# Two first products interleaved per tile of x, squares on ACT, and a third pair of output tiles ahead of the last head's transposes

## The chip, the cores and the metric

One core of a Trainium2 chip runs one launch of the kernel. The metric is the device time of a launch in microseconds, as a median of several runs. A profile is one more execution, recorded by the hardware profiler; its "span" goes from its first to its last instruction. The engines are PE (matmul and transpose), PEld (weight loads, beside PE), DVE, ACT, POOL and SP (which here only issues DMAs).

## What is computed

Two layers on 512 tokens of 1024 features, float32 (shapes fixed, one batch). Cut to what matters here:

```python
for l in range(2):
    n = rmsnorm(h, attn_norm[l])
    u, v_sgu, q, k, v_att = split(n @ w_in[l])           # 512 columns each
    y_sgu = gelu(u) * (tril(w_s) @ groupnorm(gelu(v_sgu)) + b_s)   # per chunk of 128 tokens
    y_att = diff_attention(rope(q), rope(k), v_att)      # 4 heads, two softmaxes each, then rmsnorm
    h = h + concat(y_sgu, y_att) @ w_out[l]
    h = h + (silu(conv(g)) * conv(v)) @ w_down[l]        # g, v = rmsnorm(h) @ w_up[l]; 2816 wide
return rmsnorm(h, final_norm)
```

## The kernel before

The residual lies on chip as eight tiles `hT` of [128 features, 512 tokens]. Each float32 operand of a matmul is split into a high and a low part, and each product takes three matmuls (high x high, high x low, low x high). The 1/rms of a token is applied after the product, so products can start on `g * x` before the sum of squares is known.

**Weights.** `block(i)` streams the weights in blocks of [128, 1024], two ahead (`AHEAD = 2`), through three buffers each of `raw`, `wh`, `wl`: SP's DMA into `raw`, a cast on ACT into `wh`, a subtraction on POOL (in the mixer) into `wl`. A `wh` buffer comes free when PE has finished the block before in it. Of layer 0, blocks 0 to 19 belong to `w_in`, 20 to 27 to `w_out`.

**Products.** `feat_step` multiplies one tile of x with two 128-column tiles of weights (6 matmuls of 512 columns); `tok_gemm` makes tokens the rows (12 matmuls of 256 columns per tile). `products()` is a generator, one yield per tile: gate values `vs` of groups 0 and 1 (blocks 0, 1), queries `q` (2, 3), gate values of groups 2 and 3 (4, 5), keys `k` (6, 7), attention values `va` (8, 9), and on. `run(steps, n)` takes n steps and after each the next piece of element-wise work from the queue `due`: for gate values gelu and squares on ACT, sums, a reciprocal root (`gr`, `rsqrt`) and scaling on DVE, split into `vg` parts; for q and k `rope`: shuffle and product on DVE, two POOL operations (`q_0sh`, `q_0t`), a split on ACT and DVE. All four PSUM banks of `ps_mm` turn around in these products.

**Order.** Where `pinned[0]` is true, each engine's instructions run as written; engines are coupled by semaphores alone. An engine that waits holds everything behind it.

**Opening.** `block(0)` brings x and the blocks 0 and 1 in 16 DMAs; each tile of x is scaled and split (`gh_a` on ACT, `gl_a` on DVE), its square is made and added on POOL (tiles 0 to 3) or made on ACT (4 to 7); the rotary tables are small DVE operations. Then come the sums (`norm.sums`: four transposes `ss_a`, `rcol_a` on DVE), and a row of 1/rms (`norm.rows`: `sr_a`).

**End of the mixer.** `project()` sums the first four tiles of the output projection (`pairs`, 16 steps; inputs in the order ya0, ya1, ya2, ys0 to ys3, ya3, blocks 20 to 23) between the attention units. After its 14th step the last head's output is normed on DVE (`out_norm`, tile `o`), transposed on PE (`ot`), split (`yah`, `yal`), and the rest of the steps follow. `residual` adds each finished tile to `hT` and feeds the next norm (`gh_f`, `gl_f`, square, sum), one tile after the other. Tiles 4 and 5, then 6 and 7, are two further `feat_gemm` (blocks 24, 25 and 26, 27).

Of the kernel before, what the change touches and what calls it, by code (L numbers as in the profile page):

```python
# [21 lines left out]
P = 128  # L22
# [20 lines left out]
# columns of the packed per-partition parameters  # L43
# [9 lines left out]
# 2 pi in pieces of 12 bits, so that their products with integers below 2**12 are exact  # L53
# [16 lines left out]
def trunk(ctx: ExitStack, tc, a, out):  # L70
# [24 lines left out]

    def tr_bank(name):
# [21 lines left out]
    pe, act, dve, gps = Ordered(nc.tensor), Ordered(nc.scalar), Ordered(nc.vector), Ordered(nc.gpsimd)  # L118
    mm, transpose = pe.matmul, pe.transpose

    # ---- residual stream, features on partitions
# [3 lines left out]
    # an early activation, so that the table's load is not in the way  # L125
# [4 lines left out]
    # TensorE works on zeros until the inputs come, so that its clock is up by then  # L130
# [6 lines left out]
    # ---- the weights' stream: each chunk comes once and is split into two exact parts  # L137
# [12 lines left out]
    AHEAD = 2  # L150

    def block(i):
        while len(loaded) <= min(i + AHEAD, len(specs) - 1):
# [8 lines left out]
            if j < KD // 4:  # L162
                # the first blocks come in pieces, between the tiles of x
                for k in range(4):
                    m = 4 * j + k
                    c = slice(k * 256, (k + 1) * 256)
                    nc.sync.dma_start(out=hT[m], in_=a["xT"][m])
                    nc.sync.dma_start(out=raw[:, c], in_=specs[j][:, c])
                    if m < 2:
                        dve.tensor_copy(h[:, c], raw[:, c])  # L170
                    norm.scaled(m)
                    if m >= 2:
                        act.copy(h[:, c], raw[:, c])
                    dve.tensor_sub(lo[:, c], raw[:, c], h.bitcast(F32)[:, c])
                    if m < 4:
                        norm.squared(m, True)
            else:
                nc.sync.dma_start(out=raw, in_=specs[j])
                act.copy(h, raw)
                mixer = j % (len(specs) // DEPTH) < 28  # L180
                eng = gps if mixer and j > 1 or j % 3 == 1 else dve
                eng.tensor_sub(lo, raw, h.bitcast(F32))
            loaded.append((h, lo))
        return loaded[i]

    def kept(j, n):
        """a block of the last products, which are done for one half of the tokens after the other"""
# [25 lines left out]
    def feat_gemm(banks, xs):  # L213
        """banks[j] = W[:, j]^T x; features out. Yields after each tile of x."""
# [5 lines left out]

    def tok_gemm(banks, xs):
        """x^T W for 256 columns; tokens out, two tiles of them in a bank"""
        for k, (xh, xl) in enumerate(xs):
# [3 lines left out]
            last = k == len(xs) - 1  # L227
            for t in range(NT):
                ts = slice(t * P, (t + 1) * P)
                o = banks[t // 2][:, t % 2 * 256 : t % 2 * 256 + 256]  # L230
                mm(o, xh[:, ts], h[:, c], start=k == 0 and t % 2 == 0, stop=False)
                mm(o, xh[:, ts], lo[:, c], start=False, stop=False)
                mm(o, xl[:, ts], h[:, c], start=False, stop=last and t % 2 == 1)
# [10 lines left out]
    # work on finished products, spread over the steps that follow them  # L244
# [9 lines left out]
    # ---- constants  # L254
# [9 lines left out]
    # ---- rotary tables, [feature, token]  # L264
# [5 lines left out]
    def rotary_tables():  # L270
        W = NT * HALF
        posf = sm.tile([P, NT], F32, tag="posf", name="posf", bufs=1)
        v = nc.vector
        v.tensor_copy(posf, posi)
        T = lambda n: sm.tile([P, W], F32, tag=n, name=n, bufs=1)
# [6 lines left out]
        )  # L282

        def turns(name, unit):
            k = T(name)
            v.tensor_scalar(k, r, 1.0 / (2.0 * math.pi) / unit, MAGIC, op0=ALU.mult, op1=ALU.add)
            v.tensor_scalar(k, k, MAGIC, unit, op0=ALU.subtract, op1=ALU.mult)
            return k

        def less(k, c):  # L290
            v.scalar_tensor_tensor(r, k, -TWO_PI[c], r, op0=ALU.mult, op1=ALU.add)

        k1 = turns("k1", 2.0**24)
# [25 lines left out]
        nc.scalar.activation(sn, r, AF.Sin)  # L319
        nc.scalar.activation(cs, cs, AF.Sin)  # L320
        for nm, src, dst, fill in (("c", cs, CT, 1.0), ("s", sn, ST, 0.0)):
            wide = tp.tile([P, 514], F32, tag="t", name=f"wide{nm}")[:, :S]
            nc.gpsimd.memset(wide, fill)
# [19 lines left out]
    def rsqrt(x, n, name):  # L343
        """x**-0.5 of a few columns: a guess from the exponent, then Newton's steps; x is lost"""
# [11 lines left out]
    # ---- RMS norm over features: g * h in two parts now, 1/rms of each token later  # L356
    class Norm:
# [17 lines left out]
        def squared(self, m, on_pool=False):  # L375
            sq = self.acc if m == 0 else tmp(f"sq{m}_{self.tag}")
            if on_pool:
                gps.tensor_mul(sq, hT[m], hT[m])
            else:
                act.activation(sq, hT[m], AF.Square)  # L380
            if m > 0:
                (dve if m == KD - 1 or m > 4 and self.tag == "a0" else gps).tensor_add(self.acc, self.acc, sq)

        def sums(self):
            """1/rms, a column for each tile of tokens"""
# [8 lines left out]
        def rows(self):  # L394
            """1/rms, a row on every partition"""
# [20 lines left out]
    block(0)  # L416
    for m in range(4, KD):
        norm.squared(m)
    rotary_tables()
    nc.sync.dma_start(out=par[:, C_CW:], in_=a["par"][:, C_CW:])  # L420
    for l in range(DEPTH):
        lam_init = 0.8 - 0.6 * float(np.exp(-0.3 * l))
        xs = norm.parts
        # ---- per-layer small parameters
        lamv = tmp(f"lamv{l}", 4 * HD).rearrange("p (v d) -> p v d", d=HD)
        nc.sync.dma_start(out=lamv, in_=a["lam"][l].rearrange("(v d) -> v d", d=HD).partition_broadcast(P))
        bsb = lp.tile([P, NG, P], F32, tag="bsb", name=f"bsb{l}")
        nc.sync.dma_start(out=bsb, in_=a["b_s"][l].partition_broadcast(P))
        wsp = tmp(f"wsp{l}").rearrange("p (g q) -> p g q", g=NG)
        nc.sync.dma_start(out=wsp, in_=a["w_sT"][l])  # L430

        def small():
            # lambda, on every partition
# [12 lines left out]
        # spatial weights: [q, g, p], zero where p < q  # L446
# [632 lines left out]
```

## Time and profile before

| | |
|---|---|
| median of 3 runs | 1157.69 us (1156.96 to 1157.77) |
| span of the profiled execution | 1155.4 us |
| PE busy | 1123.3 us, 97% |
| DVE, ACT, POOL busy | 685.9, 475.3, 416.3 us |

The profiled execution has no time of its own beside its span; the median of the runs is 2.3 us above it, which is what lies around a span. The rows further on start with the time in us from the span's start and the duration; a bracket at a row's end is the idle time of that engine ahead of it and what ended that. Matmuls overlap, so the distance between starts is what one costs, not its printed duration.

### The profile page before, as it was taken

What the parts mean: (1) busy time and instruction counts of PE and PEld (TensorE: products, weight loads), DVE (VectorE), ACT (ScalarE), POOL (GpSimd) and SP (SyncE); (2) the same over time, 40 slices, a digit from 0 to 9 for tenths busy, and PEclk for the clock granted to TensorE, in tenths of its full rate; (3) what the DMA queues carried; (4) which work ended last, traced back from release to release, by engine and by line L of the source; (5) the groups of instructions that cost most, each with busy time, mean ns of one, the idle gap of its engine ahead of it and who ended that gap; (6) DMA issues with size and microseconds to landing.
All of it is one profiled execution on the core that took longest, in us unless ns stands there. A gap on an engine that the chain in (4) does not pass through costs nothing.

```text
span 1155.4 us, 14800 instructions
## 1 busy us (share of the span) xinstructions
PE 1123.3 (97%) x5637; PEld 941.8 (82%) x5637; DVE 685.9 (59%) x1253; ACT 475.3 (41%) x797; POOL 416.3 (36%) x318
## 2 busy tenths in 40 slices
PE   7899998999999999999999999999999999999996
PEld 6787887888888888888889788778888888888886
DVE  8768786475665226764338688745666622565634
ACT  4345554443443223444344545544344321344351
POOL 5475423522232113143456752352323311232351
PEclk8999999999999999999999999999999999999999
DMA  6222212223323322323232211123322332233222
GB/s 206 80 73 92 73 47 72 93 92 93 108 91 99 102 91 92 109 82 91 101 106 91 92 55 56 55 73 110 106 95 91 91 110 92 91 100 101 75 90 73
DMA packets 33351, 105.24 MB, mean 91 GB/s; under 512 B 3968, under 2 KB 7424, under 8 KB 33280
## 3 DMA queue, kind: packets, MB, share of 16 engines
q1 hardware_dynamic: 32848, 104.27, 28.1%
q8 instruction: 44, 0.72, 0.3%
q14 instruction: 27, 0.22, 0.1%
q10 hardware_dynamic: 432, 0.03, 0.0%
HBM read 102.19 MB, written 2.10 MB: 90 GB/s over the span
## 4 chain that ended last, share of the span: by engine, by line
PE 80%; DVE 9%; POOL 3%; issue 3%; ACT 3%; DMA 0%; SPq 0%; DVEq 0%; POOLq 0%; ACTq 0%
PE g L116 21%; PE v L116 21%; PE dn L116 18%; PE wo L116 6%; PE u L116 4%; PE q L116 3%; PE dl L116 2%; PE sc L116 1%; PE vs L116 1%; PE mx L116 1%; PE av L116 1%; ACT wh L116 1%; DVE y L116 1%; POOL wl L116 1%; DVE s L116 1%
## 5 line engine op out<-in xcount | busy, mean ns | idle before, releaser
L116 POOL TENSOR_TENSOR wl<-raw,wh 128x1024 fp32r<-128x1024 f32 (+1 forms) x103 | 245.8, 2389 | 567.3 <-ACT wh L116 557.4
L116 ACT CAST wh<-raw 128x1024 fp32r<-128x1024 f32 (+2 forms) x200 | 198.5, 996 | 366.4 <-issue 195.1
L116 DVE TENSOR_TENSOR wl<-raw,wh 128x1024 fp32r<-128x1024 f32 (+2 forms) x99 | 123.8, 1250 | 129.0 <-ACT wh L116 129.0
L116 PE MATMUL g<-gh_f,wh 128*128 128x512 f32 x352 | 137.2, 390 | 0.0
L116 PE MATMUL v<-gh_f,wh 128*128 128x512 f32 x352 | 137.2, 390 | 0.0
L116 PE MATMUL v<-gh_f,wl 128*128 128x512 f32 x352 | 137.1, 389 | 0.0
L116 PE MATMUL g<-gh_f,wl 128*128 128x512 f32 x352 | 137.1, 389 | 0.0
L116 PE MATMUL v<-gl_f,wh 128*128 128x512 f32 x352 | 137.0, 389 | 0.0
L116 PE MATMUL g<-gl_f,wh 128*128 128x512 f32 x352 | 137.0, 389 | 0.0
L116 DVE SCALAR_TENSOR_TENSOR cv<-up_cv,par,cv 128x512 f32<-128x512 f32 x88 | 74.3, 891 | 8.0 <-ACT cv L116 7.7
L116 PEld LDWEIGHTS v<-gh_f,wl 128*128 128x128 f32 x352 | 66.1, 188 | 13.7
L116 PEld LDWEIGHTS g<-gh_f,wl 128*128 128x128 f32 x352 | 66.1, 188 | 13.7
L116 PEld LDWEIGHTS v<-gl_f,wh 128*128 128x128 f32 x352 | 66.1, 188 | 13.7
L116 PEld LDWEIGHTS g<-gl_f,wh 128*128 128x128 f32 x352 | 66.1, 188 | 13.6
L116 PEld LDWEIGHTS v<-gh_f,wh 128*128 128x128 f32 x352 | 66.1, 188 | 13.6
L116 PEld LDWEIGHTS g<-gh_f,wh 128*128 128x128 f32 x352 | 66.1, 188 | 13.6
L116 DVE SCALAR_TENSOR_TENSOR cg<-up_cg,par,cg 128x512 f32<-128x512 f32 x88 | 71.1, 855 | 6.8 <-ACT cg L116 6.3
L116 DVE TENSOR_TENSOR up_cv<-v,rstd_f 128x512 f32<-128x512 f32 x44 | 30.2, 692 | 67.5 <-PE v L116 67.5
L116 DVE TENSOR_TENSOR up_cg<-g,rstd_f 128x512 f32<-128x512 f32 x44 | 30.0, 692 | 53.7 <-PE g L116 53.1
L116 ACT ACTIVATE s<-s,mn 128x128 f32<-128x128 f32 (+3 forms) x64 | 35.5, 556 | 58.9 <-DVE mn L116 58.9
L116 DVE TENSOR_TENSOR hT<-dn,hT 128x512 f32<-128x512 f32 x28 | 19.1, 691 | 47.5 <-PE dn L116 47.5
L116 ACT ACTIVATE cg<-cg 128x512 f32<-128x512 f32 x44 | 27.7, 630 | 46.7 <-DVE cg L116 46.6
(575 smaller groups left out, 2624.2 us busy)
## 6 DMA issues: line engine op xcount, KB each, us to landing
raw<-in_w_up SPq DMA_DIRECT2D x88, 512.0 KB, 3.4
raw<-in_w_dn SPq DMA_DIRECT2D x40, 512.0 KB, 3.5
raw<-in_w_in SPq DMA_DIRECT2D x38, 512.0 KB, 3.5
raw<-in_w_out SPq DMA_DIRECT2D x16, 512.0 KB, 3.4
hT<-in_xT SPq DMA_DIRECT2D x8, 256.0 KB, 4.2
raw<-in_w_dn SPq DMA_DIRECT2D x8, 256.0 KB, 3.3
out<-y SPq DMA_DIRECT2D x8, 256.0 KB, 2.3
raw<-in_w_in SPq DMA_DIRECT2D x8, 128.0 KB, 4.1
```

The lines of the kernel that those rows point to most:

```text
L116: return lambda *args, **kw: pin(getattr(self.engine, op)(*args, **kw))
```

## The change

Four parts, the last two in both layers.

1. `opening()` replaces the split inside `block`: per tile of x three DMAs instead of two (x, a piece of block 0 or 1, a piece of block 2 or 3; 24 in all), and `both_first()` does per tile the 12 matmuls of `vs` and the 6 of `q`. Blocks 4 and 5 come after tiles 5 and 7. The second gate values use the two banks of the scores.
2. All squares of x are made on ACT and added on DVE; blocks 4 to 6 get their low part on DVE. POOL has no work on x left. The rotary table's steps are spread, two after each tile, the rest after `norm.sums`.
3. `project()` stops after 12 of 16 steps. Tiles 4 and 5 (`late`, in the scores' banks) take their first six inputs ahead of the last head's transposes; then come the last two inputs of all six tiles.
4. Only after that come the residuals: six in a row, then tiles 6 and 7.

```diff
+    def opening():
+        first = [[], []]
+        for m in range(KD):
+            sync.dma_start(out=hT[m], in_=a["xT"][m])
+            c = slice(m % 2 * 256, m % 2 * 256 + 256)
...
+            for b, (r, h, lo) in enumerate(tiles):
+                spec = specs[2 * b + m // 4]
+                sync.dma_start(out=r[:, c], in_=spec[:, m % 4 * 256 : (m % 4 + 1) * 256])
...
+            norm.squared(m)
+            if m > 0:
+                for _ in range(2):
+                    next(rotary)
+            if m == 5:
+                loaded.extend([None] * 4)
+                AHEAD[0] = 0
+                block(4)
+        block(5)
+        AHEAD[0] = 2
...
-                eng = gps if mixer and j > 1 or j % 3 == 1 else dve
+            eng = gps if (j > 6 if mixer else j % 3 == 1) else dve
...
+            def steps():
+                for k, x in enumerate(xs):
+                    tok_step(vb, x, first[0][k], k == 0, k == KD - 1)
+                    yield
+                    feat_step(qb, x, first[1][k], 0, k == 0, k == KD - 1)
+                    yield
...
+        def project_last(k):
+            for c in range(2):
+                feat_step(pairs[c], mixed[k], final[0], (2 * c + k - KD + 2) * 256, False, k == KD - 1)
...
-        run(steps, 1)
+        run(steps)
+
+        mixed = [ya[0], ya[1], ya[2], ys[0], ys[1], ys[2], ys[3], None]
+        late = [sc_bank(f"wo{4 + j}_{l}") for j in range(2)]
+        more = feat_gemm(late, mixed)
+        AHEAD[0] = 1
+        run(more, 6)
+        AHEAD[0] = 2
         end.out_turn()
         end.out_high()
         end.out_low()
-        run(steps)
+        mixed[-1] = ya[3]
+        project_last(KD - 2)
+        run(more, 1)
+        project_last(KD - 1)
         flush()
...
         for c in range(2):
             residual(c, pairs[c])
-        for c in range(2, 4):
-            banks = [mm_bank(f"wo{2 * c + j}_{l}") for j in range(2)]
-            run(feat_gemm(banks, mixed))
-            residual(c, banks)
+        run(more)
+        residual(2, late)
+        banks = [mm_bank(f"wo{6 + j}_{l}") for j in range(2)]
+        run(feat_gemm(banks, mixed))
+        residual(3, banks)
```

PE, start of layer 0, before: tile 1 of x (`gh1`) follows tile 0 (`gh0`), both for `vs` alone (`wh0`, `wl0` are the parts of block 0).

```order
L116 MATMUL vs1_0_0_289<-wh0_128,gh0_a0_133 128x256
L116 MATMUL vs1_0_0_289<-wl0_129,gh0_a0_133 128x256
L116 MATMUL vs1_0_0_289<-wh0_128,gl0_a0_134 128x256
L116 MATMUL vs0_0_0_288<-wh0_128,gh1_a0_142 128x256
L116 MATMUL vs0_0_0_288<-wl0_129,gh1_a0_142 128x256
```

The same place now (`oh1`, `ol1` are the parts of block 2):

```order
L119 MATMUL vs1_0_0_306<-oh0_0_129,gl0_a0_139 128x256
L119 MATMUL q0_0_307<-gh0_a0_138,oh1_0_132 128x512
L119 MATMUL q0_0_307<-gl0_a0_139,oh1_0_132 128x512
L119 MATMUL q0_0_307<-gh0_a0_138,ol1_0_133 128x512
L119 MATMUL q1_0_308<-gh0_a0_138,oh1_0_132 128x512
L119 MATMUL q1_0_308<-gl0_a0_139,oh1_0_132 128x512
L119 MATMUL q1_0_308<-gh0_a0_138,ol1_0_133 128x512
L119 MATMUL vs0_0_0_305<-oh0_0_129,gh1_a0_148 128x256
```

Six matmuls of the queries moved between two tiles of the gate values.

POOL, layer 0, from the turned queries to the turned keys, before (`wl9`, `wl10` are low parts of weight blocks, `wsl0` of the spatial weights):

```order
L116 TENSOR_TENSOR q0_1t1_599<-q0_1t1_599,q0_1sh_597 128x512
L116 TENSOR_TENSOR wl7_605<-raw7_603,wh7_604 128x1024
L116 TENSOR_TENSOR wl8_670<-raw8_668,wh8_669 128x1024
L116 AFFINE_SELECT wsp0_280<-wsp0_280 128x512
L116 TENSOR_TENSOR wsl0_283<-wsp0_280,wsh0_282 128x512
L116 TENSOR_TENSOR wl9_729<-raw9_727,wh9_728 128x1024
L116 TENSOR_TENSOR wl10_771<-raw10_769,wh10_770 128x1024
L116 TENSOR_TENSOR k0_0sh_787<-k0_0sh_787,Sr0_516 128x512
```

The same place now:

```order
L119 TENSOR_TENSOR wl8_670<-raw8_668,wh8_669 128x1024
L119 AFFINE_SELECT wsp0_297<-wsp0_297 128x512
L119 TENSOR_TENSOR wsl0_300<-wsp0_297,wsh0_299 128x512
L119 TENSOR_TENSOR wl9_713<-raw9_711,wh9_712 128x1024
L119 TENSOR_TENSOR q0_0sh_723<-q0_0sh_723,Sr0_618 128x512
L119 TENSOR_TENSOR q0_0t1_725<-q0_0t1_725,q0_0sh_723 128x512
L119 TENSOR_TENSOR q0_1sh_735<-q0_1sh_735,Sr0_618 128x512
L119 TENSOR_TENSOR q0_1t1_737<-q0_1t1_737,q0_1sh_735 128x512
L119 TENSOR_TENSOR wl10_765<-raw10_763,wh10_764 128x1024
L119 TENSOR_TENSOR wl11_845<-raw11_843,wh11_844 128x1024
L119 TENSOR_TENSOR k0_0sh_907<-k0_0sh_907,Sr0_618 128x512
```

The spatial weights and block 9 moved ahead of the turned queries; between queries and keys only blocks 10 and 11 are left.

ACT, end of layer 0's mixer, before (`wh26`, `wh27` are casts of weight blocks, `gh` and `sq` the feeds of the residual's tiles):

```order
L116 ACTIVATE gh2_f0_2249<-hT2_87,par_93 128x512
L116 ACTIVATE sq2_f0_2253<-hT2_87 128x512
L116 ACTIVATE gh3_f0_2257<-hT3_88,par_93 128x512
L116 ACTIVATE sq3_f0_2261<-hT3_88 128x512
L116 CAST wh26_2267<-raw26_2266 128x1024
L116 CAST wh27_2297<-raw27_2296 128x1024
```

The same place now:

```order
L119 ACTIVATE gh3_f0_2337<-hT3_88,par_93 128x512
L119 ACTIVATE sq3_f0_2341<-hT3_88 128x512
L119 ACTIVATE gh4_f0_2351<-hT4_89,par_93 128x512
L119 ACTIVATE sq4_f0_2355<-hT4_89 128x512
L119 ACTIVATE gh5_f0_2359<-hT5_90,par_93 128x512
L119 ACTIVATE sq5_f0_2363<-hT5_90 128x512
L119 CAST wh27_2369<-raw27_2368 128x1024
```

Block 27 moved from behind the feeds of four tiles to behind those of six; the casts of blocks 25 and 26 moved ahead of `yah`, and layer 1 has the same order.

## Rows read from the trace of the kernel before

**Rows 1.** The page: busy time by engine; GB/s in 40 equal slices of the span.
```profile
PE 1123.3 (97%) x5637; PEld 941.8 (82%) x5637; DVE 685.9 (59%) x1253; ACT 475.3 (41%) x797; POOL 416.3 (36%) x318
...
GB/s 206 80 73 92 73 47 72 93 92 93 108 91 99 102 91 92 109 82 91 101 106 91 92 55 56 55 73 110 106 95 91 91 110 92 91 100 101 75 90 73
```

**Rows 2.** Timeline, PE, opening of layer 0: start, duration, engine, line, operation, tiles, shape.
```profile
5.03 0.56 PE L116 MATMUL vs<-wh,gh_a 128*128 128x256 f32 x1
...
45.43 0.39 PE L116 MATMUL q<-gh_a,wl 128*128 128x512 f32 x1
...
57.17 0.40 PE L116 MATMUL k<-gh_a,wh 128*128 128x512 f32 x1
...
68.08 0.28 PE L116 MATMUL va<-wh,gh_a 128*128 128x256 f32 x1
...
80.62 0.33 PE L116 MATMUL sc<-k_0l,q_0h 64*128 64x128 f32 x2 [0.61 <-DVE k_0l L116]
...
86.30 0.59 PE L116 MATMUL sc<-k_0h,q_0h 64*128 64x256 f32 x2 [0.93 <-DVE mn L116]
```

**Rows 3.** Timeline, DVE, 14 to 28 us: one tile of x's work.
```profile
14.29 0.74 DVE L116 SCALAR_TENSOR_TENSOR gl_a<-hT,par,gh_a 128x512 fp32r<-128x512 f32 x1
14.95 0.42 DVE L116 TENSOR_TENSOR wl<-raw,wh 128x256 fp32r<-128x256 f32 x1
...
27.44 0.69 DVE L116 TENSOR_TENSOR acc_a<-acc_a,sq_a 128x512 f32<-128x512 f32 x1 [0.33 <-ACT sn L319]
```

**Rows 4.** Timeline, DVE, 38 to 80 us: from 1/rms to the split keys.
```profile
38.24 0.16 DVE L353 SCALAR_TENSOR_TENSOR rcol_a<-rcol_a0t,rcol_a 128x4 f32<-128x4 f32 x1
...
50.67 1.29 DVE L116 TENSOR_TENSOR vs<-vs,gr 128x512 f32<-128x512 f32 x2
...
67.59 2.32 DVE L352 TENSOR_TENSOR gr_1t<-gr_1t,gr 128x8 f32<-128x8 f32 x1
...
70.75 1.29 DVE L116 TENSOR_TENSOR vs<-vs,gr 128x512 f32<-128x512 f32 x2
...
79.46 1.10 DVE L116 TENSOR_TENSOR k_0l<-k_0t,k_0h 128x512 fp32r<-128x512 f32 x1 [3.56 <-ACT k_0h L116]
```

**Rows 5.** Timeline, POOL, 54 to 77 us: the turned queries and keys.
```profile
54.09 1.30 POOL L116 TENSOR_TENSOR q_0sh<-q_0sh,Sr 128x512 f32<-128x512 f32 x1 [4.88 <-DVE q_0sh L116]
...
76.11 1.29 POOL L116 TENSOR_TENSOR k_0sh<-k_0sh,Sr 128x512 f32<-128x512 f32 x1
```

**Rows 6.** Timeline, ACT, 61 us: the gelus of the second gate values.
```profile
61.24 1.56 ACT L116 ACTIVATE vs<-vs,rcol_a 128x256 f32<-128x256 f32 x4
```

**Rows 7.** Timeline, PE, end of both layers' mixers, to the FFN's first product.
```profile
185.48 0.39 PE L116 MATMUL wo<-ys_1h,wh 128*128 128x512 f32 x1
...
191.36 1.09 PE L116 MATMUL ot<-ident,o 128*128 128x128 f32 x4 [2.99 <-DVE o L116]
...
223.16 0.39 PE L116 MATMUL g<-gh_f,wh 128*128 128x512 f32 x1
...
746.58 0.39 PE L116 MATMUL wo<-ys_1h,wh 128*128 128x512 f32 x1
...
782.87 0.39 PE L116 MATMUL g<-gh_f,wh 128*128 128x512 f32 x1
```

**Rows 8.** Stretches around both waits for `o`: length, PE, PEld, DVE, ACT, POOL busy, clock.
```profile
189.00:197.00 8.00, 5.64 (x21) 4.77 (x22) 4.01 (x11) 2.34 (x3) 0.29 (x1) 0.79 0.20 66
750.00:758.00 8.00, 5.54 (x27) 4.69 (x28) 4.12 (x12) 2.26 (x3) 1.57 (x2) 1.00 0.20 66
```

**Rows 9.** Timeline, DVE, layer 0: the residual's first two tiles.
```profile
198.19 0.69 DVE L116 TENSOR_TENSOR hT<-wo,hT 128x512 f32<-128x512 f32 x1 [4.25 <-PE wo L116]
...
200.35 0.68 DVE L116 TENSOR_TENSOR hT<-wo,hT 128x512 f32<-128x512 f32 x1
```

**Rows 10.** Timeline, ACT, layer 0: the casts of blocks 26 and 27.
```profile
206.51 1.98 ACT L116 CAST wh<-raw 128x1024 fp32r<-128x1024 f32 x2
```

**Rows 11.** Timeline, POOL, layer 0: the low parts of blocks 26 and 27.
```profile
208.00 4.76 POOL L116 TENSOR_TENSOR wl<-raw,wh 128x1024 fp32r<-128x1024 f32 x2
```

More of the change, by code (lines that the diff above doesn't have):

```diff
@@ L94, in mm_bank, with sc_bank @@
         return ps_mm.tile([P, S], F32, tag="mm", name=name)
+    def sc_bank(name):
+        return ps_sc.tile([P, S], F32, tag="sc", name=name)
     def tr_bank(name):
@@ L161, in block @@
             lo = wp.tile([P, 1024], F32R, tag="wl", name=f"wl{j}")[:, :n]
[L162 to L180, printed above, removed]
-                eng = gps if mixer and j > 1 or j % 3 == 1 else dve
-                eng.tensor_sub(lo, raw, h.bitcast(F32))
+            (sync if j < 6 else nc.sync).dma_start(out=raw, in_=specs[j])
@@ L219, in feat_gemm, with tok_step @@
             yield
+    def tok_step(banks, x, w, first, last):
+        (xh, xl), (h, lo) = x, w
+        for t in range(NT):
+            ts = slice(t * P, (t + 1) * P)
+            o = banks[t // 2][:, t % 2 * 256 : t % 2 * 256 + 256]
+            mm(o, xh[:, ts], h, start=first and t % 2 == 0, stop=False)
+            mm(o, xh[:, ts], lo, start=False, stop=False)
+            mm(o, xl[:, ts], h, start=False, stop=last and t % 2 == 1)
     def tok_gemm(banks, xs):
-        for k, (xh, xl) in enumerate(xs):
+        for k, x in enumerate(xs):
             if k % 4 == 0:
@@ L226, in tok_gemm @@
             c = slice(k % 4 * 256, (k % 4 + 1) * 256)
[L227 to L233, printed above, removed]
+            tok_step(banks, x, (h[:, c], lo[:, c]), k == 0, k == len(xs) - 1)
             yield
@@ L415, in trunk @@
     pinned[0] = True
[L416 to L420, printed above, removed]
+    rotary = rotary_tables()
+    first = opening()
+    sync.dma_start(out=par[:, C_CW:], in_=a["par"][:, C_CW:])
     for l in range(DEPTH):
@@ L512, in trunk, with gate_values @@
         vg, us, ya, ys = [None] * 2, [None] * NG, [None] * NH, [None] * NG
-        def gate_values(gp):
-            banks = [mm_bank(f"vs{b}_{gp}_{l}") for b in range(2)]
-            yield from tok_gemm(banks, xs)
+        def gate_values(gp, banks, steps):
+            yield from steps
             gs = sm.tile([P, 8], F32, tag="gs", name=f"gs{l}_{gp}", bufs=2)
@@ L612, in scores @@
                 qsl = slice(n - P, n)
[L613 removed]
+                bk = [sc_bank(f"sc{self.name}_{c}") for c in range(2)]
                 for x, y, st, en in ((qh, kh, True, False), (qh, kl, False, False), (ql, kh, False, True)):
@@ L721, in products @@
             yield from project()
-        pairs = []
+        pairs, final = [], []
         def project():
             pairs.extend([mm_bank(f"wo{2 * c + j}_{l}") for j in range(2)] for c in range(2))
-            for k0 in range(0, KD, 2):
+            for k0 in range(0, KD - 2, 2):
                 w = next_block()
@@ L738, in trunk @@
         steps = products()
-        run(steps, 8)
-        due.extend([nothing, nothing])
-        run(steps, 2)
-        norm.sums()
-        run(steps, 3)
-        norm.rows()
-        run(steps, 2)
-        if l == 0:
-            rotary_turn()
+        if l == 0:
+            run(steps, 16)
+            due.extend([nothing] * 4)
+            norm.sums()
+            for _ in rotary:
+                pass
+            run(steps, 4)
+            norm.rows()
+            run(steps, 2)
+            rotary_turn()
+        else:
+            run(steps, 8)
+            due.extend([nothing, nothing])
+            run(steps, 2)
+            norm.sums()
+            run(steps, 3)
+            norm.rows()
+            run(steps, 2)
         Cr, Sr = fslot(f"Cr{l}"), fslot(f"Sr{l}")
@@ L750, in trunk @@
         dve.tensor_mul(Sr, ST, norm.rstd)
-        run(steps, 13)
+        run(steps, 28 - (22 if l == 0 else 15))
         spatial()
         run(steps, 12)
+        flush()
         nlam, sgain = small()
```

116 lines of the change are left out of this document (75 added, 41 removed).

## The prediction

> **What bounds the kernel now.** First the page's busy times: PE works 1123.3 of 1155.4 us [rows 1], so what is to be won is idle PE time, 32 us, and PE time at the lower clock. Second, PE's timeline, where the idle time stands: in the opening of layer 0 and in the wait for the last head's normed output `o`, 2.99 us [rows 7]. A 512-column matmul costs (68.08 - 57.17) / 48 = 0.227 us, a 256-column one (57.17 - 45.66) / 96 = 0.120 us, 45.66 being one matmul behind the last `q` [rows 2]. The first two products hold 96 of one and 48 of the other, 22.4 us, but run from 5.03 to 45.66 [rows 2]. That seems to offer 18 us. Third, how PE comes to the first scores: there it waits for the split keys, only 0.61 us, and soon 0.93 us for the row minima [rows 2]. The keys are the end of a chain of element-wise work from 1/rms at 38.4 to `k_0l` at 80.56 [rows 4]. So two chains arrive together at 80.6, PE's and this one, and the opening is worth what the later of them gains.
>
> **The opening, on PE.** All of a tile's operands are early. DVE needs per tile 0.74 + 2 x 0.42 + 0.69 [rows 3] and two small steps of 0.2 (from 69.91, the end of one, to 70.75 stand four [rows 4]), 2.7 us, against 12 x 0.120 + 6 x 0.227 = 2.8 us on PE: PE sets the pace, just. The squares left POOL, so no POOL operation holds up DVE there. The eight more DMAs and blocks 2 to 4 put 4.7 MB ahead of the end of tile 7; at the 206 GB/s of the first slice [rows 1] that takes 23 us, and PE comes to tile 7 at 25. I count 0.5 us for the start: the two products end at 5.0 + 0.5 + 22.4 = 27.9. The sums' transposes (0.4), the second gate values (11.5), `sr` and the two table transposes (1.2) bring the keys to 41.0, the values to 51.9, and PE to the scores at 63.4, 17 us earlier than before.
>
> **The opening, on the element-wise chain.** Work that only moves costs what it costs before; what matters is what stands in its way. The table's last steps now alternate with those of 1/rms, which hides them (two chains of 0.2 us steps, each waiting for itself): 1/rms is there at 32, and it is not the limit. The limit is PE's release of weight buffers: the cast of block 8 waits for the end of block 5, at 41.0, its POOL operation runs 42.0 to 44.4 (half of 4.76 [rows 11]) and shuts DVE's small steps out, as a step of the size of `rcol`, 0.16 us, was stretched to 2.32 [rows 4]. Ten of these remain: the first gate values are scaled at 46.6, against 50.67 [rows 4]. Then the turned queries: before, POOL took them up 54.09 - 50.67 = 3.42 us later [rows 4, 5]. Now block 9 stands ahead of them, and its cast behind three 512-wide ACT operations: 46.6 + 0.7 + 3 x 0.6 + 1.0 + 2.4 = 52.5. (1.0 and 2.4 are halves of the pairs in [rows 10, 11].) If block 9 could be passed it would be 50.0; as queues run in order, I take 52.5. From there to the second gelus 61.24 - 54.09 = 7.15 as before [rows 5, 6]: 59.7. They stay behind the split queries on ACT. From the gelus to the scaled second values it was 70.75 - 61.24 = 9.51 [rows 4, 6], with three POOL pieces on the way; now there is one, block 11. The two that left cost about a 512-wide POOL operation, 1.3 [rows 5]: 8.2, so 67.9. From these to POOL's start on the keys it was 76.11 - 70.75 = 5.36, behind block 10 [rows 4, 5]; now nothing is queued there, and the 3.42 of the queries holds: 71.3. From there to the scores 80.62 - 76.11 = 4.51 [rows 2, 5]: **75.8**. So PE stands idle for 12 us ahead of the first score, and the opening wins 80.6 - 75.8 = 4.8 us, not 17. Bounds: 73.1 without block 9 ahead of the queries, 78.2 if one more POOL operation of 2.4 us shuts DVE out. After that wait PE starts at half its clock; I take 1.4 us for that (below). The 0.93 us wait at 86.30 [rows 2] goes, since a slower PE comes later to it. Net gain 4.8 + 0.9 - 1.4 = **4.3 us**.
>
> **The end of the mixer, in each layer.** Counted from the first matmul of `ys_1` (185.48 and 746.58), the rest of the output projection takes 37.68 us in layer 0 and 36.29 in layer 1 [rows 7]. It holds 144 matmuls, 32.7 us, and a transpose, 0.4. Removed is the wait for `o`, 2.99 us in both: 60 matmuls instead of 12 stand ahead of the transposes now, which PE reaches at 13.6, and `o` is there at 191.36 - 185.48 = 5.9. That would be worth 4.6 and 3.2 us if nothing came in its place. Something does. On ACT and POOL block 27 now stands behind the feeds of six tiles instead of four, and the feeds start later. The first bank is complete after 60 matmuls, the transpose and 18 + 3 more, at 19.0. The residual's tiles follow each other every 200.35 - 198.19 = 2.16 us [rows 9], since each adds on DVE, scales on ACT and splits on DVE in turn: the sixth at 29.8. Before, the cast of block 26 came 1.84 us and its POOL work 3.33 us after the fourth tile's add at 204.67 [rows 9 to 11]; block 27 takes that place now: cast from 31.6 to 32.6, POOL until 29.8 + 3.33 + 2.38 = 35.5. PE needs it after 120 matmuls and the transpose, at 27.7 for the cast part and 28.1 for the low part. It waits 4.9 us, does two matmuls, and waits again until 35.5. The 22 matmuls left end at 40.5. So layer 0 loses 40.5 - 37.7 = **2.8 us**, layer 1 40.5 - 36.3 = **4.2 us**, before the clock. Blocks 25 and 26 come in time: the cast of 26 waits for the end of block 24 at 10.9 and is needed at 22.2. Nothing else covers this: PE's queue behind block 27 holds the last two tiles, and behind them the FFN.
>
> **The clock.** The two waits for `o` before are equal, yet the granted clock was 0.79 in the 8 us around one and 1.00 around the other, for the same busy time [rows 8]; 0.79 is a mean of the levels 1.2 and 2.4 GHz. The layers differ by 37.68 - 36.29 = 1.39 us [rows 7], which I take as the price of one return from 1.2 GHz. The new waits are longer (12 us once, 7.3 us with two matmuls inside twice), so I charge it three times: once in the 4.3 above, and 2.8 in the mixers. The Trainium skill ("TensorE: Matmul & The Clock Gate", Part 1) says that the half clock is the default and that sustained work lifts it. By that rule all three waits pay; the stretch of layer 1 shows that a wait of 3 us can go unpunished [rows 8], so the sum without it is a rival.
>
> **The sum.** -4.3 + 2.8 + 4.2 + 2.8 = +5.5 us on the profiled execution's span of 1155.4: 1160.9. The runs' median is 2.3 us above the span, the same launch around it: **1163.2 us**.
>
> **Rivals.** (1) *No clock lost.* All three waits end at full clock: -5.7 + 7.0 = +1.3, 1159.0. Against it: the 0.79. (2) *The opening wins less.* One more lock of DVE, or ACT held by a late cast: 78.2 instead of 75.8, so 1165.6. (3) *The change does what it says in the mixer*, block 27 in time: -4.6 - 3.2, with the opening -4.3: 1145.6, faster. It decides where the low part of block 27 is done by 28.1 after the first `ys_1`; for that the feeds would have to run at 0.7 us per tile, and they show 2.16. (4) *PE sets the opening.* Scores at 63.4 need the chain to shorten by another 12 us: -17.2 + 9.8 = -7.4, 1150.3, faster. Against it: every piece of it keeps its place on ACT behind the casts. (5) The opening starves for data: this delays PE's 63.4, which has 12 us of slack, so it costs little.
>
> **How the numbers follow.** Forecast as summed 0.52, rival 1 0.21, rival 2 0.14, rival 3 0.06, rival 4 0.07. A measurement here tells about 0.2%, 2.3 us, from no change: faster is below 1155.4, slower above 1160.0. Rivals 3 and 4 are faster, 0.13; rival 1 is the same, 0.21; the rest is slower, 0.66. The range takes in rival 1 with a us of the chain's lower bound, and rival 2 with a us: 1158 to 1167, which leaves out rivals 3 and 4 and some tails.
>
> **What the new profile would show.** Right: PE without gaps from 5 to about 63; then one wait of about 12 us at the first scores, ended by ACT's `k_0h` or DVE's `k_0l`, at 74 to 78; no wait at `ot`; in both layers a wait of about 5 us, two matmuls, and one of 2.4 us, ended by ACT's `wh` and POOL's `wl`, in the fifth input of the last two output tiles; half clock behind each. Wrong: scores before 70, or no wait in the last output tiles, or gaps among the first 16 steps over 3 us in all.

## The result, and the profile after

The changed kernel takes 1166.32 us (median of 4 runs, 1164.18 to 1166.4), the kernel before 1157.73 (4 runs); the ratio is 1.0066, with an interval of 1.0048 to 1.0084. It is slower by 8.6 us, 3.1 us more than forecast and inside the range given. The profiled execution took 1166.31 us with a span of 1164.6, against a span of 1155.4; in every execution the time is about 1.7 us above the span.

PE does the same work, and that is the first line to see: 1123.8 us busy against 1123.3 [rows 1]. The difference is idle time, and the page's sums don't show where it is. Nor do they show an exchange: from 10 to 40 us PE ran at a granted clock of 0.83, 0.66 and 0.83 before, in steps of 10 us, and runs at 1.00 now; the lower level stands behind the new waits instead.

```profile
PE 1123.8 (96%) x5637; PEld 941.4 (81%) x5637; DVE 675.9 (58%) x1267; ACT 478.3 (41%) x808; POOL 395.0 (34%) x305
```

PE's list of waits does: what it waited for, then us in total, times, the longest.

```profile
PE sc L119 <- ACT k_0h L119: 11.1, 1, 11.1
PE wo L119 <- ACT wh L119: 9.8, 2, 4.9
PE wo L119 <- POOL wl L119: 3.2, 2, 1.6
```

None of the three is in the kernel before; its 2.99 us waits for `o` [rows 7] are gone. PE's timeline gives their places: the end of the two first products, the first scores, and in each layer the first `ys_1`, the two waits in the last output tiles and the FFN's first product.

```profile
28.76 0.60 PE L119 MATMUL ss_a<-ident,acc_a 128*128 128x128 f32 x4
...
75.62 0.47 PE L119 MATMUL sc<-k_0h,q_0h 64*128 64x128 f32 x2 [11.05 <-ACT k_0h L119]
76.74 0.47 PE L119 MATMUL sc<-k_0l,q_0h 64*128 64x128 f32 x2 [0.65 <-DVE k_0l L119]
77.95 0.63 PE L119 MATMUL q<-gl_a,wh 128*128 128x512 f32 x1
...
182.73 0.39 PE L119 MATMUL wo<-ys_1h,wh 128*128 128x512 f32 x1
...
215.44 0.79 PE L119 MATMUL wo<-ys_1h,wh 128*128 128x512 f32 x1 [4.88 <-ACT wh L119]
218.25 0.80 PE L119 MATMUL wo<-ys_1h,wl 128*128 128x512 f32 x1 [1.58 <-POOL wl L119]
...
225.23 0.39 PE L119 MATMUL g<-gh_f,wh 128*128 128x512 f32 x1
...
748.71 0.39 PE L119 MATMUL wo<-ys_1h,wh 128*128 128x512 f32 x1
...
781.45 0.79 PE L119 MATMUL wo<-ys_1h,wh 128*128 128x512 f32 x1 [4.89 <-ACT wh L119]
784.24 0.80 PE L119 MATMUL wo<-ys_1h,wl 128*128 128x512 f32 x1 [1.57 <-POOL wl L119]
...
791.52 0.39 PE L119 MATMUL g<-gh_f,wh 128*128 128x512 f32 x1
```

Between the milestones of [rows 2, 7] and these the whole difference of the spans can be booked:

| stretch | before | after | change | forecast |
|---|---|---|---|---|
| start to first `ys_1`, layer 0 | 185.48 | 182.73 | -2.75 | -4.3 |
| to the FFN, layer 0 | 37.68 | 42.50 | +4.82 | +4.2 |
| FFN and next layer, to its `ys_1` | 523.42 | 523.48 | +0.06 | 0 |
| to the FFN, layer 1 | 36.29 | 42.81 | +6.52 | +5.6 |
| from there to the end | 372.53 | 373.08 | +0.55 | 0 |
| span | 1155.4 | 1164.6 | +9.2 | +5.5 |

The forecast's column has the clock's share where it was charged. The signs and the order of the terms came as forecast; all are a little worse.

Behind the waits PE runs at its lower level: a 512-column matmul takes 0.427 us from start to start (six of them from 219.27 to 221.83) instead of 0.227. The windows (columns as in [rows 8]) begin at the first matmul behind the second wait of each layer, and the first one covers the six us behind the scores:

```profile
76.74:82.74 6.00, 6.00 (x17) 4.73 (x18) 2.99 (x14) 4.87 (x12) 2.82 (x2) 0.53 0.00 1
218.25:225.23 6.98, 6.98 (x22) 5.60 (x23) 1.50 (x2) 0.00 (x0) 3.25 (x1) 0.71 0.65 200
784.24:791.52 7.28, 7.28 (x23) 5.87 (x23) 1.51 (x2) 0.00 (x0) 3.25 (x1) 0.68 0.59 214
```

0.53, 0.71 and 0.68 are mixtures of 1.2 and 2.4 GHz, and PE is busy all through, so this time is in none of the waits. The Trainium skill ("TensorE: Matmul & The Clock Gate", Part 1) has the half clock as the default that activity lifts; by that rule all three waits pay, and the trace agrees with these three numbers.

### The profile page after: what moved, and what is told of

The parts are those of the page before. It is cut to its first block, busy times and chain, and to the rows that moved or that the text cites. A ratio compares the mean times of both kernels' runs of the same rounds, so it can differ in the third digit from the quotient of the medians.

```text
span 1164.6 us, 14820 instructions
## 1 busy us (share of the span) xinstructions
PE 1123.8 (96%) x5637; PEld 941.4 (81%) x5637; DVE 675.9 (58%) x1267; ACT 478.3 (41%) x808; POOL 395.0 (34%) x305
## 4 chain that ended last, share of the span: by engine, by line
PE 83%; DVE 6%; POOL 4%; ACT 3%; issue 3%; DVEq 0%; POOLq 0%; ACTq 0%
PE g L119 21%; PE v L119 21%; PE dn L119 18%; PE wo L119 6%; PE u L119 4%; PE q L119 3%; PE vs L119 3%; PE dl L119 2%; PE sc L119 1%; POOL wl L119 1%; PE av L119 1%; PE mx L119 1%; ACT wh L119 1%; DVE s L119 1%; DVE hT L119 1%
## 5 line engine op out<-in xcount | busy, mean ns | idle before, releaser
L119 POOL TENSOR_TENSOR wl<-raw,wh 128x1024 fp32r<-128x1024 f32 (+1 forms) x98 | 235.0, 2400 | 584.3 <-ACT wh L119 574.5
L119 ACT CAST wh<-raw 128x1024 fp32r<-128x1024 f32 (+1 forms) x192 | 194.0, 1016 | 373.2 <-issue 189.2
L119 DVE TENSOR_TENSOR wl<-raw,wh 128x1024 fp32r<-128x1024 f32 (+1 forms) x94 | 120.2, 1279 | 129.4 <-ACT wh L119 129.2
L119 ACT ACTIVATE s<-s,mn 128x128 f32<-128x128 f32 (+3 forms) x64 | 35.5, 557 | 61.1 <-DVE mn L119 61.1
L119 ACT ACTIVATE cg<-cg 128x512 f32<-128x512 f32 x44 | 27.8, 631 | 46.6 <-DVE cg L119 46.6
```

Source lines behind the costliest of these rows:

```text
L119: return lambda *args, **kw: pin(getattr(self.engine, op)(*args, **kw))
```

## Experiments

**One part at a time.** Two kernels split the change. The first keeps the opening and has the ends of both mixers as before; the second has the opening of before and the new ends.

```diff
 # opening alone: the changed kernel, with
-        late = [sc_bank(f"wo{4 + j}_{l}") for j in range(2)]
-        more = feat_gemm(late, mixed)
...
+        run(steps, 1)
         end.out_turn()
```

> The changed kernel with parts 3 and 4 undone: only the opening is the new one, the ends of both mixers are those of before. Theory (the element-wise chain from 1/rms to the split keys sets the opening): the first `ys_1` of layer 0 came 2.75 us earlier in the changed kernel (182.73 against 185.48), so this kernel takes 1157.7 - 2.75 = 1155.0 us (1154.0 to 1156.0), PE waits about 11 us at the first scores, for `k_0h`, and the 2.99 us wait for `o` is there in both layers. Rival (the opening alone frees PE, and what stood against it came from the ends of the mixers): 1142 to 1150 us.

Measured 1154.15 us, ratio 0.9961 (0.9948 to 0.9975). PE waits 11.0 us for `k_0h`, and 3.0 us for `o` in each layer.

```diff
 # new ends alone: the kernel before, with
-        run(steps, 1)
+        run(steps)
+        late = [sc_bank(f"wo{4 + j}_{l}") for j in range(2)]
+        more = feat_gemm(late, mixed)
...
```

> The kernel before with parts 3 and 4 alone: the opening is that of before, the third pair stands ahead of the last head's transposes in both layers. Theory (block 27 is cast behind the feeds of six tiles; the clock falls behind the wait): both ends take what they take in the changed kernel, 42.5 and 42.8 us from the first `ys_1` to the first `g` against 37.68 and 36.29, so 1157.7 + 4.8 + 6.5 = 1169.0 us (1168 to 1170.5), with the same pair of waits of 4.9 and 1.6 us in each layer. Rival (the late block comes from the new opening's shift of the weight buffers, which part 3 alone does not have): no such waits, 1150 to 1154 us.

Measured 1169.6 us, ratio 1.0094 (1.0076 to 1.0113), with the same pair of waits:

```profile
218.78 0.80 PE L119 MATMUL wo<-ys_1h,wh 128*128 128x512 f32 x1 [4.88 <-ACT wh L119]
221.56 0.79 PE L119 MATMUL wo<-ys_1h,wl 128*128 128x512 f32 x1 [1.56 <-POOL wl L119]
```

The two halves, -3.9 and +11.6 us against their own runs of before, add up to +7.7 where the whole has +8.6. To within a us, then, the change is a small gain and a larger loss that don't touch each other, and the loss needs nothing of the opening.

**Is it block 27's place?** Its request moves ahead of the residuals, and nothing else changes:

```diff
+        AHEAD[0] = 1
+        block(nxt[0])
+        AHEAD[0] = 2
         for c in range(2):
             residual(c, pairs[c])
         run(more)
```

> The changed kernel with block 27 requested after the last inputs of the first four tiles, ahead of the residuals: its cast stands on ACT ahead of the feeds of six tiles, its low part on POOL ahead of their sums. Theory (block 27 is late only for its place behind the feeds): its buffer comes free when block 23 is done, at about 19 us after the first `ys_1`, cast and low part are there at about 23, PE comes to it at 27.7. No wait, no half clock: both ends take 144 matmuls and the transposes, 33.1 us, instead of 42.5 and 42.8: 1166.3 - 9.4 - 9.7 = 1147.2 us (1146 to 1150). Rival 1 (its data or its buffer are late, not its place): the waits stay, 1164 to 1168. Rival 2 (the cast and POOL's 2.4 us ahead of the feeds push the feeds so far that the FFN's first product waits for the last ones): the waits go but PE waits 2 to 5 us in the FFN's first products, 1150 to 1157.

Measured 1156.68 us (0.9981, 0.9969 to 0.9993 of before). The waits for `wh` and `wl` are gone and so is rival 1: data and buffer were there. But 9.5 us of the hoped 19 are missing: the ends take 37.5 us each, not 33.1. PE's, DVE's, ACT's and POOL's timelines, in this order, show the waits that came up instead:

```profile
207.99 0.56 PE L119 MATMUL wo<-yah,wh 128*128 128x512 f32 x1 [2.47 <-DVE hT L119]
...
221.64 0.74 PE L119 MATMUL g<-gh_f,wl 128*128 128x512 f32 x2 [0.66 <-POOL wl L119]
```

```profile
204.99 2.33 DVE L119 SCALAR_TENSOR_TENSOR gl_f<-hT,par,gh_f 128x512 fp32r<-128x512 f32 x1 [2.83 <-ACT gh_f L119]
207.25 0.68 DVE L119 TENSOR_TENSOR hT<-wo,hT 128x512 f32<-128x512 f32 x1
208.72 0.75 DVE L119 SCALAR_TENSOR_TENSOR gl_f<-hT,par,gh_f 128x512 fp32r<-128x512 f32 x1 [0.79 <-ACT gh_f L119]
```

```profile
203.28 1.05 ACT L119 CAST wh<-raw 128x1024 fp32r<-128x1024 f32 x1 [5.91 <-PE wo L119]
204.24 0.72 ACT L119 ACTIVATE gh_f<-hT,par 128x512 fp32r<-128x512 f32 x1
```

```profile
204.41 2.37 POOL L119 TENSOR_TENSOR wl<-raw,wh 128x1024 fp32r<-128x1024 f32 x1 [7.56 <-ACT wh L119]
```

Block 27 now stands ahead of the first feed on both engines. On ACT its cast waits for its buffer until 203.28, and `gh_f`, behind it, starts at 204.24: DVE is idle 2.83 us ahead of `gl_f` instead of 0.79, so 2.0 us later. On POOL its low part falls on that feed: `gl_f` takes 2.33 us instead of 0.75, so another 1.6, and ends 0.5 us behind POOL's operation. The add of the second tile is queued behind `gl_f` on DVE, and only that add frees the bank in which tile 6 is to be summed. PE waits for it at tile 6's first input. Behind that wait the granted clock is 0.86 for 12 us:

```profile
207.99:219.91 11.92, 11.92 (x46) 9.70 (x47) 6.37 (x10) 8.08 (x12) 7.20 (x6) 0.86 0.10 39
```

The second rival came true: cast and low part push the feeds, but the main wait is at another place than it said (the bank of tile 6; the FFN waits only 0.66 us). The expectation of the next kernel names POOL's share alone; ACT's is the larger. That POOL shuts out a DVE step that reads two operands from SBUF is what the Trainium skill ("SBUF — State Buffer", section "Who interferes with whom") states, and the trace agrees: 2.33 us here, while the adds to `hT`, with one operand in PSUM, keep 0.68 beside POOL's sums (at 209.39, beside one from 209.28 that takes 1.34).

**The same with the bank and block 28 seen to.** Both adds of a pair come ahead of its feeds, block 27 behind two feeds, block 28 behind `more`:

```diff
+            for j in range(2):
+                dve.tensor_add(hT[2 * c + j], banks[j], hT[2 * c + j])
             for j in range(2):
-                m = 2 * c + j
-                dve.tensor_add(hT[m], banks[j], hT[m])
-                norm.feed(m)
+                norm.feed(2 * c + j)
...
-        for c in range(2):
-            residual(c, pairs[c])
+        residual(0, pairs[0])
+        AHEAD[0] = 1
+        block(nxt[0])
+        AHEAD[0] = 2
+        residual(1, pairs[1])
         run(more)
+        block(nxt[0])
         residual(2, late)
```

> The changed kernel with both adds of a residual pair ahead of its two feeds, block 27 requested after the first pair's feeds (two tiles instead of six ahead of it on ACT and POOL), and block 28, the FFN's first, after the third pair's last product. The kernel with block 27 ahead of all feeds lost the waits for it, but POOL's low part (204.41, 2.37 us) held up DVE's `gl_f` (2.33 instead of 0.75 us), which stood ahead of the add that frees the bank of tile 6: PE waited 2.47 us there and 0.66 us for block 28. Theory (that is all that was left): no wait over 0.5 us in either end, each 33.1 to 33.8 us from the first `ys_1` to the first `g`, 1166.3 - 9.1 - 9.4 = 1147.8 us (1146.5 to 1150). Rival (whatever stands between the feeds, the residual's chain of 2.16 us per tile and POOL's two low parts of 2.4 us end later than PE needs them): the wait comes up in the FFN's first product at `gh_f` or `gl_f`, 1151 to 1157 us.

Measured 1152.16 us (0.9941, 0.9924 to 0.9959). Both ends, from the first `ys_1` to the first `g`, are now solid matmuls, 33.13 and 33.14 us at full clock:

```profile
182.54:215.67 33.13, 33.13 (x149) 27.43 (x148) 20.57 (x30) 14.60 (x21) 17.99 (x9) 1.00 0.22 66
...
741.70:774.84 33.14, 33.14 (x150) 27.42 (x148) 20.58 (x30) 14.61 (x21) 18.00 (x9) 1.00 0.22 67
```

The third part of the change can do what it says, then: 4.55 and 3.15 us less than before. What is missing to 1147.8 is the next thing in line, in the list of PE's waits:

```profile
PE ss_f L119 <- DVE acc_f L119: 4.8, 2, 2.4
```

The FFN's norm takes its sum of squares after six steps of the first product, and DVE's last sum is now 2.4 us later than PE. The clock adds to it in the profiled execution (1153.71): from `ss_f` to the second product it takes 229.60 - 226.37 = 3.23 us in layer 0 and 790.25 - 785.54 = 4.71 in layer 1, 1.5 us more at the lower level. So neither text was right on this kernel: the ends are as the theory said, and the wait came behind them at the sums, not at `gh_f` or `gl_f`.

**The clock by itself.** PE gets something to do in the opening's wait:

```diff
+        if l == 0:
+            filler = tr_bank("filler")
+            for _ in range(46):
+                mm(filler, zeros[:, :P], zeros, start=True, stop=True)
```

> The changed kernel with 46 matmuls on zeros (bfloat16, 512 columns, into a free bank, added work that nothing reads) on PE ahead of layer 0's first scores, some 10 us in the 11 us wait. Theory (the wait also costs the clock behind it): the scores start when the keys are there, at 76.7 as before, but at full clock; from there to the first `ys_1` 104.0 us instead of 106.0, in all 1166.3 - 2.0 = 1164.3 us (1163.8 to 1164.8). Rival (the clock costs nothing, the slow matmuls behind the wait are made up by a later wait): 1166.3 us, no difference. Both have the two waits in the ends of the mixers as in the changed kernel.

Measured 1164.84 us (1163.18 to 1165.21, 5 runs), 1.5 us under the changed kernel. The runs of the two kernels overlap (1164.18 to 1166.4 there), so the price rests on the traces. In the profiled execution (1163.18) the matmuls behind the scores start at full pace (0.23 apart):

```profile
63.66 10.10 PE L119 MATMUL filler<-zeros 128*128 128x512 bf16 x46
74.87 0.33 PE L119 MATMUL sc<-k_0h,q_0h 64*128 64x128 f32 x2 [1.10 <-ACT k_0h L119]
75.99 0.33 PE L119 MATMUL sc<-k_0l,q_0h 64*128 64x128 f32 x2 [0.80 <-DVE k_0l L119]
...
76.70 0.39 PE L119 MATMUL q<-gl_a,wh 128*128 128x512 f32 x1
76.93 0.39 PE L119 MATMUL q<-gh_a,wl 128*128 128x512 f32 x1
...
179.99 0.39 PE L119 MATMUL wo<-ys_1h,wh 128*128 128x512 f32 x1
```

From the last scores' operand to the first `ys_1` it is 179.99 - 75.99 = 104.00 us, against 182.73 - 76.74 = 105.99. The clock behind the 11 us wait costs 1.99 us. That the operand is there 0.75 us earlier is not the filler's doing: the two first products end 0.75 us earlier too, at 28.01 instead of 28.76.

**Is the opening bound by a chain or by its order?** PE's order is left alone; in layer 0 the second gate values' gelus move up on ACT, the keys' turn up on DVE and POOL, what is left of the gate values goes behind the scores, and blocks 10 and 11 get their low parts on DVE:

```diff
+            if l == 0 and gp == 1:
...
+                due.extendleft([lambda: (gelu(1), square(0), square(1)), partial(gelu, 0)])
+                due.extend([reduced, nothing])
+                early["vs"] = [roots, nothing, both, parts]
+                return
...
+            if l == 0 and at == 0 and name == "q":
+                due.extend(work[:2])
+            elif l == 0 and at == 0:
+                q = early["q"]
+                due.extend(work[:2] + [lambda: (q[2](), q[3]()), lambda: (work[2](), work[3]())])
...
             yield from values(0)
+            due.extend(early.pop("vs", []))
```

> The changed kernel with layer 0's element-wise work in another order: the second gate values' gelus and squares directly behind the first ones' squares on ACT, the keys' shuffles and products on DVE directly behind the queries', the second gate values' roots, scaling and split among the first attention units; low parts of blocks 10 and 11 on DVE. PE's order is the same. Theory (PE waits 11 us for a chain that was queued in this order, not for an engine's throughput): POOL ends the queries at 59.4 as now and takes the keys at once, first turned key 62.0, split keys 63.8; PE comes at 63.4. The wait is 0 to 2 us, the half clock goes with it: 1166.3 - 12 - 2 = 1152.3 us (1151 to 1156). Rival (the work that is put off, 6 us of DVE, comes back as waits for row minima and split parts in the first attention units): the first scores at 64 to 65, but only 5 to 8 us won, 1158 to 1161 us.

Measured 1156.76 us (0.9985, 0.9972 to 0.9997). The first scores come at 64.66, 12.1 us earlier, and PE waits 0.37 us there. Then both texts are partly right: from there to the first `ys_1` (172.82) it takes 108.2 us instead of 104.0, and of these 4.2 us 3.7 are idle time of PE (6.0 us in this stretch instead of 2.3), which stands in the first units:

```profile
64.66 0.33 PE L119 MATMUL sc<-k_0l,q_0h 64*128 64x128 f32 x2 [0.37 <-DVE k_0l L119]
...
70.07 0.59 PE L119 MATMUL sc<-k_0h,q_0h 64*128 64x256 f32 x2 [0.67 <-DVE mn L119]
...
73.32 0.30 PE L119 MATMUL at<-ident,s 128*128 128x128 f32 x1 [0.86 <-DVE s L119]
...
79.61 0.41 PE L119 MATMUL at<-ident,s 128*128 128x128 f32 x2 [0.94 <-DVE s L119]
...
93.04 0.66 PE L119 MATMUL at<-ident,s 128*128 128x128 f32 x4 [1.90 <-DVE aTl L119]
```

Of 12.1 us on the scores and 2 us of clock, 9.6 arrive at the end. The edit changes two things at once, the order and the engine of two low parts, and no run separates them.

**Both.** The two edits together:

> Both of these edits in one kernel. Theory (the two places are independent): the gains add, 1166.3 - 14 - 18.5 = 1133.8 us (1132 to 1139), under both kernels by over 18 us. Rival (what is won ahead of the attention is lost ahead of the last head's transposes, where `o` then comes late): PE waits at `ot` in layer 0, 1139 to 1146 us.

Measured 1143.54 us (0.9869, 0.9844 to 0.9893). The theory's 1133.8 was too hopeful by what the two kernels above had given back: 14.2 and 9.6 us are 23.8, and 1166.3 - 23.8 = 1142.5. `ot` has no wait for `o`, so its rival fell too; the gains add as measured.

**The sums of squares two steps later,** which takes up the 2.4 us found above:

```diff
-                    run(steps, 6)
-                    norm.sums()
                     run(steps)
-                    run(more, 1)
+                    norm.sums()
+                    run(more, 3)
                     norm.rows()
```

> The kernel with both edits, and the sums' transposes of the FFN's norm put two steps later (behind all eight steps of the FFN's first product instead of six), the row of 1/rms behind three steps of the second instead of one. In the kernel with both edits PE waits 2.4 us in each layer at these transposes (`ss_f`) for DVE's `acc_f`: with the ends of the mixers shorter, the last sum of squares comes later than PE. Theory (that wait is all that is left of them, two steps of 1.36 us cover it): 1143.5 - 4.8 = 1138.7 us (1137.5 to 1140). Rival (1/rms is late, the convolution behind it frees the banks later, and PE waits there instead): 1141 to 1144 us.

Measured 1138.1 us, ratio 0.9829 (0.9812 to 0.9847): as the theory had it, and 20.0 us under the kernel before in the same comparison. The wait at `ss_f` is gone, and 0.2 us at `sr_f` is all that came in its place.

**The first attention units cleared.** In one more kernel `small()` runs behind the queries' turn, the second key tile's split behind the first minima, and the gate values' end after `queries(1)`:

```diff
+        if l == 0:
+            run(steps, 2)
+            nlam, sgain = small()
...
+        if l == 0:
+            due.append(early["k"][3])
...
-            due.extend(early.pop("vs", []))
             yield from queries(1)
+            due.extend(early.pop("vs", []))
```

> The same, and layer 0's first attention units cleared: the sums of lambda and the exponential's table on ACT 13 us earlier (behind the queries' products on DVE), the split of the second key tile behind the first row minima, block 11's low part on POOL, the second gate values' roots, scaling and split eight steps later. In the kernel with the reordered element-wise work alone the first row minima were at 69.9, 5 us behind the first scores at 64.7, and PE waited 0.67, 0.86, 0.94 and 1.90 us in the first units; from the first scores to the first `ys_1` it took 108.2 us, against 104.0 with the clock kept up. Theory (these waits are the work put off, and it can be put where nobody waits): about 3 of the 4 us come back, 1138.7 - 3 = 1135.7 us (1134 to 1138). Rival (PE's waits there come from POOL's low parts shutting DVE out, in whichever place): no difference to the kernel beside it, within 1.5 us.

Measured 1138.08 us (1136.94 to 1139.32), no difference. PE's busy time between 60 and 100 us, first in the kernel beside it, then in this one, says why the theory was plausible:

```profile
60.00:80.00 20.00, 17.20 (x99) 13.45 (x97) 13.54 (x40) 9.66 (x21) 10.79 (x7) 1.00 0.17 53
80.00:100.00 20.00, 18.07 (x97) 13.88 (x98) 17.91 (x48) 11.03 (x32) 10.20 (x6) 1.00 0.23 79
```

```profile
60.00:80.00 20.00, 19.35 (x110) 15.36 (x108) 15.15 (x35) 10.42 (x25) 13.77 (x8) 1.00 0.24 79
80.00:100.00 20.00, 19.70 (x120) 15.50 (x120) 18.21 (x50) 9.74 (x27) 10.73 (x7) 1.00 0.17 54
```

There 35.3 of 40 us became 39.0, so these waits went. But the first `ys_1` came only 173.16 - 171.90 = 1.3 us earlier, and 0.6 of that is the opening (the two first products end at 28.09 instead of 28.66). A new wait of 1.84 us for `aTl` stands at 103. PE's, DVE's and POOL's rows:

```profile
103.19 0.44 PE L119 MATMUL at<-ident,s 128*128 128x128 f32 x2 [1.84 <-DVE aTl L119]
```

```profile
99.50 1.95 DVE L686 SCALAR_TENSOR_TENSOR cf<-esum,cf,nlam 128x1 f32<-128x1 f32 x1
```

```profile
99.04 2.39 POOL L119 TENSOR_TENSOR wl<-raw,wh 128x1024 fp32r<-128x1024 f32 x1 [7.44 <-ACT wh L119]
```

A DVE step on one column, 0.22 us elsewhere (as at 107.35), took 1.95 us beside POOL's low part, and `s` and `aTl` are queued behind it. So here the rival has the mechanism as well as the number: POOL's low part shuts DVE out in the next place. In the kernel beside it one of the four waits had the same cause: a step of 0.17 us took 2.27 at 77.03, beside a low part from 76.88, ahead of the wait of 0.93 us at 80.03. Behind the new wait the granted clock is 0.72 for 6 us. How much of what is left is DVE's load (busy 18 of the 20 us up to 100 in both kernels) and how much POOL's operations beside it, was not tried. The median shows nothing of the 1.3 us: the four runs lie between 1136.94 and 1139.32, further apart than the gain.

## Why the prediction was right, point by point

1. **Which chain sets the opening: right.** PE went through without gaps and then waited 11.05 us for `k_0h`, forecast 12. Its pace was 2.82 us per tile, forecast 2.8. The step that was off is the start: I had allowed 0.5 us, but PE's first tile went at half pace to 7.3 (256-column matmuls 0.21 apart, not 0.12) and took 4.74 to 9.03, 4.3 us instead of 2.8, so the two products ended at 28.76, not 27.9, and everything released by PE shifted with it (the cast of block 8 first, at 42.19, behind a wait for PE). This differs from execution to execution: in the nine profiled with this opening the two products ended between 28.01 and 28.76. The chain's milestones, forecast and measured:

| | forecast | measured |
|---|---|---|
| 1/rms | 32 | 32.6 |
| first gate values scaled (DVE) | 46.6 | 47.55 |
| queries on POOL | 52.5 | 53.74 |
| second gelus (ACT) | 59.7 | 60.87 |
| second gate values scaled | 67.9 | 68.89 |
| keys on POOL | 71.3 | 72.30 |
| scores | 75.8 | 76.74 |

   From the second line on the difference stays between 0.9 and 1.2 us: each link has the length that [rows 4 to 6] gave it. POOL shutting out DVE's small steps was where I put it, 1.3 us later; DVE's and POOL's rows:

```profile
43.41 2.32 DVE L382 TENSOR_TENSOR gr_0t<-gr_0t,gr 128x8 f32<-128x8 f32 x1
```

```profile
43.31 2.40 POOL L119 TENSOR_TENSOR wl<-raw,wh 128x1024 fp32r<-128x1024 f32 x1 [4.60 <-ACT wh L119]
```

2. **That the order makes this chain: argued then, shown now,** but for the share of two low parts. The same work in another order, with the low parts of blocks 10 and 11 on DVE, had the scores at 64.66, where PE's own 63.4 was forecast. Rival 4 (PE sets the opening) fell for this kernel and describes the reordered one.

3. **The end of the mixer: right to 0.1 us, up to the clock.** Forecast after the first `ys_1`: the cast at 32.6, the low part at 35.5. Measured: 215.44 - 182.73 = 32.71 and 218.25 - 182.73 = 35.52. ACT and POOL show the places, block 27 behind six feeds and their sums (in both rows the blocks behind it are in the same group):

```profile
214.36 2.92 ACT L119 CAST wh<-raw 128x1024 fp32r<-128x1024 f32 x3
```

```profile
215.82 5.67 POOL L119 TENSOR_TENSOR wl<-raw,wh 128x1024 fp32r<-128x1024 f32 x2
```

   That this queue is the cause, and not data or buffers, is shown by the kernel that moves the request.

4. **The clock: right that it falls three times, too small a price.** I took 1.4 us from the difference of the two layers before. Behind the low part 22 matmuls should take 5.0 us; they took 225.23 - 218.25 = 6.98 and 791.52 - 784.24 = 7.28, so 2.0 and 2.3 us, and behind the scores it was 1.99. This term was mis-sized by 0.6 + 0.6 + 0.9 us. Rival 1 (no clock lost) is out. That the long waits pay was no luck: all eight ends with the pair of waits, in four kernels, take 42.2 to 43.1 us.

5. **The sum.** Of the 3.7 us between +5.5 and +9.2 on the span, 0.94 are the chain's late start, 2.1 the clock behind the three waits, 0.55 the stretch behind layer 1's mixer, where I expected nothing, 0.1 the rest. The 0.55 stand in the last 7 us, behind a wait of the same size in both kernels, first before, then now:

```profile
1148.92 0.43 PE L116 MATMUL sc_last<-ident,rcol_last 128*128 128x128 f32 x2 [1.74 <-DVE rcol_last L116]
```

```profile
1157.56 0.69 PE L119 MATMUL sc_last<-ident,rcol_last 128*128 128x128 f32 x2 [1.74 <-DVE rcol_last L119]
```

   Up to there both take the same from the FFN's first product (366.05 and 366.04 us). Behind it the granted clock is 0.58 before and 0.50 now, and DVE starts on the output 1.15 instead of 0.69 us after this row: all but 0.1 us of it is the clock again, at a place that the change doesn't touch. On the median the miss is only 3.1 us because another term was too large: I added 2.3 us for what lies around a span, and it is 1.7. Rival 2 named 1165.6, near the result, but not for its reason: no further lock of DVE and no late cast came into the chain.

6. **Rival 3, the gain in the mixer,** did not come about in this change, and was within reach: it needed block 27 at 28.1 after the first `ys_1`. I had looked for it in the feeds' pace (0.7 us per tile). An earlier request alone brings the block in time, while the adds to `hT` still follow each other every 2.14 us behind the second (207.25, 209.39, 211.53); to make the gain of it took the bank and block 28 as well.

## What to carry to other kernels

Moving matmuls ahead of a wait moves every buffer request that hangs on their place in the program: ask for each weight block which feeds now stand ahead of its cast, on each engine, and request it where its buffer comes free. When a wait goes, price the next two behind it as well: here the earlier block held up a bank, and behind the bank stood a sum of squares. And an opening in which PE and the element-wise work end together can only be shortened on both, so look at the order of the element-wise queue before moving matmuls.

## What the runs showed of the hardware

Waits of the same size were answered differently by the clock. Twice 2.38 us for `acc_f` in one trace (the kernel with the bank and block 28 seen to), and the 6 us behind each, in layer 0 and in layer 1 (the granted clock is the third number from the end):

```profile
226.38:232.38 6.00, 6.00 (x31) 5.02 (x32) 4.05 (x15) 1.64 (x2) 0.00 (x0) 1.00 0.28 90
785.54:791.54 6.00, 6.00 (x22) 4.98 (x23) 2.66 (x13) 1.01 (x1) 0.00 (x0) 0.74 0.28 89
```

So it was with the two waits of 2.99 us before [rows 8], and with shorter ones: in the 6 us behind 1.84 us it was 0.72 (at 103.19, first attention units cleared), behind 1.90 us 1.00 (at 93.47, the kernel beside it). What sets them apart, the traces don't show. What a return costs is the number of matmuls done at 0.427 instead of 0.227 us, about 0.2 us each: nine slow ones lost 2.0 us behind layer 0's low part (218.25 to 222.26), eleven 2.3 us behind layer 1's (784.24 to 789.02), and the 1.4 us that I read before are five and the four transposes. And a tile at half pace can stand in a stretch with a granted clock of 1.00: so it was in the first tile (4.74 to 9.02), where only the distances of the matmuls show it.
